# Ten dependent steps of a reciprocal root kept together on the vector engine by a list scheduler, and the load of the vector c moved ahead of that of x

## The chip, the core and the metric

The kernel runs on one core of one Trainium2 chip. TensorE (PE) multiplies, VectorE (DVE) and ScalarE (ACT) work on elements, GpSimd (POOL) takes some of the element work too, and SyncE (SP) issues every DMA. The metric is the device time of one execution in microseconds, the median of several runs.

## What is computed

Two transformer blocks of two layers each, one after the other, for 512 tokens of 1024 features in fp32. The first has two gated feed-forward parts around a mixer (sliding-window attention, a linear recurrence, a short convolution); the second has latent attention and then neighbourhood attention over tokens and a context, each with a convolutional feed-forward part. Every part is preceded by a norm over the features, and the shifts, scales and gates around it are products of the vector c with large matrices. Two of the norms, cut to what matters:

```python
def rmsnorm(x, g):
    xf = x.astype(jnp.float32)
    y = xf * lax.rsqrt(jnp.mean(xf * xf, axis=-1, keepdims=True) + EPS)
    return (y * g.astype(jnp.float32)).astype(x.dtype)

def first_block(x, c, w_mod, b_mod, g_norm, ...):
    c_act = jax.nn.silu(c)
    for l in range(DEPTH):
        mod = (c_act @ w_mod[l] + b_mod[l]).reshape(c.shape[0], N_MOD, D_MODEL)
        h = modulate(x, g_norm[l, 0], mod[:, 0], mod[:, 1])
        x = x + 0.5 * mod[:, 2][:, None, :] * swiglu(h, w_ffn1_gu[l], w_ffn1_down[l])
        ...

def layer_norm(x, g, b):
    mu = jnp.mean(xf, -1, keepdims=True)
    var = jnp.mean(jnp.square(xf - mu), -1, keepdims=True)
    return ((xf - mu) * lax.rsqrt(var + LN_EPS)).astype(x.dtype) * g + b
```

## The kernel before

Features lie along the 128 partitions and tokens along the free axis, so x is eight tiles of 128 by 512. Each fp32 matrix is split into a high and a low part (`wh` written by ACT, `wl` by DVE; in the same way `hh`, `hl` for activations), and each product is three matmuls. The weights come by DMA in blocks of 128 by 512 (`wr`), and the rows of the matrices that are multiplied by c come as `mr`.

The program isn't issued as it is written. `Recorder` takes it down op by op and `schedule` makes a list schedule from estimated costs: each engine takes the earliest op of the program whose operands are there and whose tiles have room. `emit` then issues all ops in that order (line 429 in the profile), and on the chip each engine runs its own list strictly in order. DVE and ACT are `PATIENT`: they leave a ready op alone for a moment if an op that stands earlier in the program becomes ready within `WAIT`, 70 ns of the schedule's clock. The schedule lets 135 ns pass between a DVE op and a DVE op that uses its result.

A norm is made for half of the tokens at a time (256; in a few places all 512). Sums over the features go through PE (`ps<-ones,acc`), then DVE has the variance `v` of each token as a column of 128 by 2 (or 4). `rsqrt` works on these columns in ten steps, each of which needs the one before: a first guess by integer arithmetic, and three Newton rounds of three ops. In the profile they are the DVE rows `c<-c` and `c<-c,c` (first the one with int32). PE then turns the column over and spreads it (`ps<-ident,c`, `bcast`), and DVE multiplies x by it. I call the ten steps a chain; the program has 27 of them, and they are numbered in order of time. In the second block's layer norms the mean is subtracted too: `x<-x,bm`, of eight tiles three on DVE and five on POOL. PE's list also holds other products, which lie before and behind the transposes of a norm as the schedule has them.

At the start, `setup` loads the eight tiles of x, then c in two halves spread over the partitions (`load_c`, tiles `b_c`, with a Silu on ACT), then the constants; `first_mods` multiplies the first rows of the matrices by c on DVE and POOL.

Of the kernel before, what the change touches and what calls it, by code (L numbers as in the profile page):

```python
# [69 lines left out]


def parts(T):
    """The tokens in halves: a norm over one runs beside the products of the other."""
    return [slice(i, i + C) for i in range(0, T, C)]


# [9 lines left out]


class View:
    """A part of a tile that gets its memory once the order of the program is known."""

    __slots__ = ("t", "box", "ops", "flat", "raw", "size")

# [37 lines left out]


class Op:
    __slots__ = ("eng", "calls", "acc", "cost", "func", "deps", "after", "succ", "begun", "need", "ready", "news", "frees", "prio", "start")


class Engine:
# [13 lines left out]


class Recorder:
    """Takes the program down op by op, then issues it in the order of a list schedule: each engine
    runs the earliest op of the program whose operands are there and whose tiles have room."""

    ENGINES = ("tensor", "vector", "scalar", "gpsimd", "sync")
    LAT = {"tensor": {"tensor": 0},
# [4 lines left out]
    FROM_PE, FROM_DMA, DMA_LAT, FREE, TO_DMA = 200, 130, 2000, 100, 300  # L162
    LOOK, LOOK_DMA = 1400, 600
    PATIENT, WAIT, SHORT = ('vector', 'scalar'), 70, 1000

    def __init__(self, nc, pools):
        self.nc, self.pools = nc, pools
        self.ops = []
        self.open = None
        self.pe = self.ve = 0.0  # L170
        self.later = 0
        for e in self.ENGINES:
            setattr(self, e, Engine(self, e))

# [32 lines left out]
    def call(self, eng, method, a, k):  # L207
        also = [(v, True) for v in k.pop("also", ())]
        outs = [a[0]] + [k[x] for x in ("accum_out",) if x in k]
        ins = [x for x in list(a[1:]) + [v for n, v in k.items() if n != "accum_out"] if isinstance(x, View)]  # L210
        acc = [(v, True) for v in outs if isinstance(v, View)] + [(v, False) for v in ins] + also
        func = a[2] if method == "activation" else None
        item = (method, a, k)
        cost = self.cost(eng, method, a, k)
        if eng == "tensor":
            self.pe += cost
        elif eng == "vector":
            self.ve += cost
        if self.open is not None:
            if self.open:  # L220
                o = self.open[0]
                o.calls.append(item)
                o.acc += acc
                o.cost += cost
                return
        o = Op()
        o.eng, o.calls, o.acc, o.cost, o.func = eng, [item], acc, cost, func
        o.prio = len(self.ops) + self.later
        if self.open is not None:
            self.open.append(o)  # L230
        self.ops.append(o)
# [53 lines left out]
    def schedule(self):  # L285
# [69 lines left out]
        while remaining:  # L355
            for e in self.ENGINES:
                if busy[e]:
                    continue
                f = future[e]
                while f and f[0][0] <= now:  # L360
                    offer(heapq.heappop(f)[2])
                best = None
                for h in avail[e].values():
                    if h and (best is None or h[0] < best[0]) and room(h[0][1], ops[h[0][1]]):
                        best = h
                if best is None or e in self.PATIENT and any(
                        r <= now + self.WAIT and p < best[0][0] and ops[i].cost < self.SHORT for r, p, i in f[:8]):
                    continue
                pick = heapq.heappop(best)[1]
                o = ops[pick]  # L370
                for g in [g for t in o.news for g in t.tags]:
                    live[g] += 1
                    if pick > cursor:
                        load[g][cursor:pick] += 1
                cost = o.cost
                if o.func is not None:
                    s = ACT_SETS.get(o.func)
                    if s is not None and s != table:
                        if not (s == "exp" and table == "sig" and o.func == AF.Tanh):
                            table = s  # L380
                            cost += 1300
                o.start = now
                order.append(pick)
                busy[e] = True
                for j in o.begun:
                    release(j, now)
                seq += 1
                heapq.heappush(events, (now + cost, seq, pick, 0))
# [41 lines left out]


class Lag:
    """Puts the parts of a chain that wait for other engines behind the start of the next ones."""

    def __init__(self, n):
        self.n, self.q = n, []
# [17 lines left out]
class Core:  # L454
# [45 lines left out]
    def setup(self):  # L500
# [7 lines left out]
        nc.vector.memset(mean, 1.0 / D)  # L508
        nc.scalar.copy(self.mean, mean)
        self.cb = {}  # L510
        self.x = []
        for m in range(KD):
            t = self.t(s="x")
            self.nc.sync.dma_start(t, self.io["xT"][m * P:(m + 1) * P, :])
            self.x.append(t)
        self.load_c(0, "c")
        self.gn = self.load_const("gnorm")
        self.bmod = self.load_const("bmod")
        self.mods = self.cst([P, 264], "mods")
# [104 lines left out]
                    self.mcol[(kind + sfx, l, ch)] = cols  # L624

    def first_mods(self):
        """The first shift and scale, finished block by block of features."""
        nc = self.nc
        Sh, G = self.mods[:, 0:8], self.mods[:, 8:16]
        for m in range(8):  # L630
# [86 lines left out]

    def rsqrt(self, v, n):
        nc = self.nc
        y, q = self.col(n), self.col(n)  # L720
        nc.vector.tensor_scalar(y.bitcast(I32), v.bitcast(I32), -0.5, float(0x5F3759DF), op0=ALU.mult, op1=ALU.add)
        for _ in range(3):
            nc.vector.tensor_tensor(q, y, y, op=ALU.mult)
            nc.vector.scalar_tensor_tensor(q, q, -0.5, v, op0=ALU.mult, op1=ALU.mult)
            nc.vector.scalar_tensor_tensor(y, q, 1.5, y, op0=ALU.add, op1=ALU.mult)
        return y

    def bcast(self, col, T, copy=None):
# [6 lines left out]
        return copy[:, :T]  # L735

    def times(self, p, c):
        """Weights of a softmax times their sum's reciprocal."""
        self.nc.gpsimd.tensor_scalar(p, p, c, 1.0, op0=ALU.mult, op1=ALU.mult)

    def rms(self, x, T, width, eps=1e-6):
# [65 lines left out]
        yield from self.ffn_end(x, dn, prev, hid, gate, T, after)  # L807

    def ffn_end(self, x, dn, prev, hid, gate, T, after):
        """The products with the last two groups of hidden features, for half the tokens and then the others."""  # L810
        gate = self.mod(*gate)
        last = len(FF_CHUNKS) - 1
        a, b = {}, {}
# [39 lines left out]
        return o  # L853

    def run(self, main, side):
        """Takes main down; between its steps, a step of the modulations for every `every` ns of tensor
        work and steps of side up to `share` of main's tensor work."""
        rec = self.nc
        mods, own = BEGIN, 0.0
        due = 0.0  # L860
# [15 lines left out]
            mark = rec.pe  # L876

    def rms_part(self, l, sub):
        """The modulated norm before a sublayer of the first block, for some of the tokens at a time."""
        out = [self.pair(S, "h") for _ in range(KD)]  # L880

        def part(sl):
# [7 lines left out]
        return out, part  # L890

    def final_part(self):
        """The first block's last norm, then the second block's first modulation."""
        nc = self.nc
        out = [self.pair(S, "a") for _ in range(KD)]
        g = self.gn[:, 48:56]
# [189 lines left out]
                yield from after(sl)  # L1086

    def stack(self, hi, lo):
        """For two heads' halves of 64 rows: each head's high and low parts over one another."""
        nc = self.nc  # L1090
        n = hi.width()
        other = self.t(F32R, s="st")[:, :n]
# [3 lines left out]
        return hi, other  # L1096

    def twice(self, hi):
        """For two heads' halves of 64 rows: each head's rows two times over."""
        nc = self.nc  # L1100
        n = hi.width()
        other = self.t(F32R, s="tw")[:, :n]
# [3 lines left out]
        return hi, other  # L1106

    def mm2x(self, outs, qs, ks, lows):
        """Products of two heads: q's both parts with k's high part in one pass, its high part with
        k's low part in the other."""  # L1110
        te = self.nc.tensor
        rows = (slice(0, 64), slice(64, 128))
        self.nc.group()
        for o, q, k in zip(outs, qs, ks):
            te.matmul(o, q, k, start=True, stop=False)
        for o, q, r in zip(outs, qs, rows):
            te.matmul(o, q[r], lows[r], start=False, stop=True)
        self.nc.group()
# [64 lines left out]
        return output  # L1183

    def centre(self, x, T):
        """Shifts each token by about the mean of its features: a layer norm, which follows, is the
        same for any shift, and its variance loses no digits to a large mean."""
        nc = self.nc
        acc = self.total(x, T, dt=F32R)
        bc = self.ps()[:, :T]  # L1190
# [2 lines left out]
            nc.vector.tensor_tensor(x[k], x[k], bc, op=ALU.subtract)  # L1193

    def ln_part(self, xs, T, l, which, kind, mod, perm=False):
        """A layer norm, and the modulation after it, for some of the tokens at a time."""
        nc = self.nc
        n = C // P
        c0 = (l * 2 + which) * 16
# [61 lines left out]
        return View(b[0][0].t, (0, P, 0, 512)), View(b[0][1].t, (0, P, 0, 512)), b[0][2]  # L1261

    def values(self, cn, wv, ts):
        """Values of 8 heads for 128 tokens: for each head its high and low parts side by side, the
        other way round for odd heads, so that the high parts' rows are the head's own."""
        nc = self.nc
        pv = self.ps()
        for k in range(2):
# [267 lines left out]
            nc.sync.dma_start(View(self.rpbt.t, (0, 16 * P, 24 * cq, 24 * cq + 24), raw=out), View(ed.t, ed.box, raw=inp))  # L1536

    def na_values(self, g, a, ac):
        """Values of two pairs of heads, tokens along the partitions: the four blocks of the latent
        tokens, the three that lie half a block further, and the context's two."""  # L1540
        nc = self.nc
        ws = [self.wblk("nqkv", 12 * g + i) for i in range(4)]
        wide = [tuple(View(w[j][part].t, (0, P, j * P, j * P + 256), (("__getitem__", ((slice(0, P), slice(j * P, j * P + 256)),), {}),))
# [282 lines left out]
```

## Time and profile before

| | |
|---|---|
| median of three runs | 3641.77 us (3635.7 to 3643.74) |
| span of the profiled execution, first to last instruction | 3637.0 us |
| PE busy | 3507.4 us, 96% of the span |
| DVE busy | 2715.5 us, 75% |
| ACT busy | 1822.0 us, 50% |
| POOL busy | 794.7 us, 22% |
| DMA | 469.86 MB, 129 GB/s on average |

For the profiled execution the page gives the span alone; it lies 4.8 us under the median of the runs and within their spread. PE's share is an average: in the slices of the page it lies at nine tenths nearly everywhere but at the start. DVE has stretches with no idle time beside long ones with a third of it. PE waits where another engine's result is late, and the rows name that engine.

### The profile page before, as it was taken

Reading aid. Unit: us, or ns where it says so; the run is one execution under the profiler, and the core shown is the slowest. Engines: PE = TensorE matmul, PEld = TensorE weight load, DVE = VectorE, ACT = ScalarE, POOL = GpSimd, SP = SyncE. Lnnn points to the kernel's source line nnn. Section 1 sums busy time; section 2 is a strip of 40 time slices with the busy share of each in tenths; the row PEclk is TensorE's granted clock in tenths of the full one; section 3 lists DMA queues with packets and bytes.
Section 4 is the critical chain, followed back from the end, with each engine's and each line's share of the span. In section 5 each row is a group of like instructions: output and inputs, shape, how many; then the busy total and the mean of one; then the engine's idle time right before and its main releaser. Section 6 shows DMA issues by size and latency. Waiting matters only on the chain.

```text
span 3637.0 us, 56958 instructions
## 1 busy us (share of the span) xinstructions
PE 3507.4 (96%) x19814; PEld 3057.1 (84%) x19814; DVE 2715.5 (75%) x5566; ACT 1822.0 (50%) x3939; POOL 794.7 (22%) x848
## 2 busy tenths in 40 slices
PE   6999999999999999999999999999999899989998
PEld 5888979878898879889888988888888888878887
DVE  8966799976597776986444589998667767786566
ACT  5434466455455644754333479785344444454332
POOL 3301142421022330230000034342000523240002
PEclk9999999999999999999999999999999999989999
DMA  9954254655356543553335322124333133233320
GB/s 316 312 157 148 82 184 148 218 182 162 103 191 197 187 132 119 193 160 116 105 108 143 107 59 58 48 68 133 110 96 105 53 100 85 76 94 103 98 87 24
DMA packets 272127, 469.86 MB, mean 129 GB/s; under 512 B 39136, under 2 KB 53472, under 8 KB 271840
## 3 DMA queue, kind: packets, MB, share of 16 engines
q1 hardware_dynamic: 271840, 466.23, 41.9%
q8 instruction: 156, 2.56, 0.3%
q14 instruction: 131, 1.07, 0.1%
HBM read 448.81 MB, written 5.50 MB: 125 GB/s over the span
## 4 chain that ended last, share of the span: by engine, by line
PE 79%; DVE 13%; issue 2%; ACT 2%; DMA 2%; POOL 1%; SPq 0%; POOLq 0%; DVEq 0%; ACTq 0%
PE ps L429 79%; DVE wl L429 2%; DVE c L429 2%; DVE mr L429 1%; DVE acc L429 1%; DVE x L429 1%; DVE mj L429 1%; DVE ptl L429 1%; DMA mr<-in_wmod 1%; POOL P L429 0%; DMA wr<-in_gu 0%; DVE pl L429 0%; DVE al L429 0%; POOL pc L429 0%; DVE yl L429 0%
## 5 line engine op out<-in xcount | busy, mean ns | idle before, releaser
L429 DVE TENSOR_TENSOR wl<-wr,wh 128x512 fp32r<-128x512 f32 (+1 forms) x1182 | 834.4, 729 | 163.0 <-ACT wh L429 134.1
L429 ACT CAST wh<-wr 128x512 fp32r<-128x512 f32 (+1 forms) x1182 | 676.6, 614 | 96.0 <-PE ps L429 61.2
L429 PE MATMUL ps<-hh,wh 128*128 128x512 f32 (+1 forms) x1864 | 692.9, 372 | 3.3 <-ACT wh L429 2.7
L429 PE MATMUL ps<-hl,wh 128*128 128x512 f32 (+1 forms) x1864 | 689.7, 370 | 6.3 <-DVE hl L429 6.2
L429 PE MATMUL ps<-hh,wl 128*128 128x512 f32 (+1 forms) x1864 | 688.0, 369 | 0.1
L429 PE MATMUL ps<-fh,wh 128*128 128x512 f32 (+1 forms) x1344 | 463.5, 345 | 0.0
L429 PE MATMUL ps<-fl,wh 128*128 128x512 f32 (+1 forms) x1344 | 462.0, 344 | 0.2 <-DVE fl L429 0.2
L429 PE MATMUL ps<-fh,wl 128*128 128x512 f32 (+1 forms) x1344 | 461.8, 344 | 0.0
L429 PEld LDWEIGHTS ps<-hl,wh 128*128 128x128 f32 x1864 | 355.4, 191 | 65.0 <-DVE hl L429 9.3
L429 PEld LDWEIGHTS ps<-hh,wh 128*128 128x128 f32 x1864 | 355.5, 191 | 60.8 <-ACT wh L429 3.1
L429 PEld LDWEIGHTS ps<-hh,wl 128*128 128x128 f32 x1864 | 355.1, 190 | 59.7 <-DVE wl L429 1.3
L429 DVE SCALAR_TENSOR_TENSOR x<-ps,mods,x 128x512 f32<-128x512 f32 (+1 forms) x400 | 254.9, 641 | 187.8 <-PE ps L429 186.1
L429 PE MATMUL ps<-ah,wh 128*128 128x512 f32 (+1 forms) x1000 | 366.9, 367 | 0.0
L429 PE MATMUL ps<-al,wh 128*128 128x512 f32 (+1 forms) x1000 | 365.3, 365 | 0.1
L429 PE MATMUL ps<-ah,wl 128*128 128x512 f32 (+1 forms) x1000 | 364.9, 365 | 0.0
L429 POOL TENSOR_TENSOR mr<-mr,b_c 128x512 f32<-128x512 f32 x123 | 179.0, 1457 | 515.1 <-DMA mr<-in_wmod 247.6
L429 DVE SCALAR_TENSOR_TENSOR cv<-ps,ffc,cv 128x511 f32<-128x511 f32 (+1 forms) x264 | 173.3, 659 | 143.7 <-ACT cv L429 140.1
L429 PEld LDWEIGHTS ps<-fl,wh 128*128 128x128 f32 x1344 | 254.7, 190 | 30.0 <-DVE fl L429 0.4
L429 PEld LDWEIGHTS ps<-fh,wl 128*128 128x128 f32 x1344 | 254.6, 189 | 30.1
L429 PEld LDWEIGHTS ps<-fh,wh 128*128 128x128 f32 x1344 | 254.7, 189 | 29.5
L429 ACT ACTIVATE cv<-ps,ffc 128x512 f32<-128x512 f32 (+1 forms) x132 | 93.4, 708 | 314.7 <-PE ps L429 314.0
L429 ACT CAST fh<-s 128x512 fp32r<-128x512 f32 x132 | 81.8, 621 | 299.1 <-DVE s L429 297.0
(332 smaller groups left out, 7115.6 us busy)
## 6 DMA issues: line engine op xcount, KB each, us to landing
wr<-in_gu SPq DMA_DIRECT2D x352, 256.0 KB, 2.9
mr<-in_wmod SPq DMA_DIRECT2D x288, 256.0 KB, 4.2
wr<-in_fin SPq DMA_DIRECT2D x264, 256.0 KB, 2.7
mr<-in_wada SPq DMA_DIRECT2D x192, 256.0 KB, 3.6
wr<-in_dn SPq DMA_DIRECT2D x176, 256.0 KB, 3.1
wr<-in_fout SPq DMA_DIRECT2D x132, 256.0 KB, 2.7
wr<-in_win SPq DMA_DIRECT2D x64, 256.0 KB, 3.3
wr<-in_nqkv SPq DMA_DIRECT2D x48, 256.0 KB, 2.9
```

The source lines that it names most:

```text
L429: getattr(eng, method)(*a, **k)
```

## The change

`rsqrt` marks its ops as urgent. Where an op of the engine's own list will be ready soon, the schedule waits for it up to 260 ns if it is urgent, and 70 ns otherwise. All urgent ops are DVE's, so ACT's own choices are made by the same rule as before. In `setup` the call of `load_c` stands ahead of the loads of x. Some comments are gone as well, by which line 429 becomes 433.

```diff
     PATIENT, WAIT, SHORT = ('vector', 'scalar'), 70, 1000
+    URGENT = 260
...
         o.prio = len(self.ops) + self.later
+        o.urgent = self.urgent
...
                 if best is None or e in self.PATIENT and any(
-                        r <= now + self.WAIT and p < best[0][0] and ops[i].cost < self.SHORT for r, p, i in f[:8]):
+                        r <= now + (self.URGENT if ops[i].urgent else self.WAIT) and p < best[0][0] and ops[i].cost < self.SHORT
+                        for r, p, i in f[:8]):
                     continue
...
         self.cb = {}
+        self.load_c(0, "c")
         self.x = []
         for m in range(KD):
             t = self.t(s="x")
             self.nc.sync.dma_start(t, self.io["xT"][m * P:(m + 1) * P, :])
             self.x.append(t)
-        self.load_c(0, "c")
...
     def rsqrt(self, v, n):
         nc = self.nc
+        nc.urgent = True
         y, q = self.col(n), self.col(n)
         nc.vector.tensor_scalar(y.bitcast(I32), v.bitcast(I32), -0.5, float(0x5F3759DF), op0=ALU.mult, op1=ALU.add)
         for _ in range(3):
             nc.vector.tensor_tensor(q, y, y, op=ALU.mult)
             nc.vector.scalar_tensor_tensor(q, q, -0.5, v, op0=ALU.mult, op1=ALU.mult)
             nc.vector.scalar_tensor_tensor(y, q, 1.5, y, op0=ALU.add, op1=ALU.mult)
+        nc.urgent = False
         return y
```

Over the whole program 144 other DVE instructions stood between the first and the last step of the 27 chains; now 19 do (4 in the first chain, 6 each in chains 7 and 18, 3 in two others). What this does to DVE's list is shown at chain 26, in the last layer norm, for the first half of the tokens. Here `c_39358` is the variance, `c_39367` the root as it comes, `c_39371` the helper; `x` are tiles of x, `bm` the mean, `ps_...` with `mods` a product that is added to x. Before:

```order
L429 TENSOR_TENSOR x_98<-x_98,bm_39369 128x256
L429 SCALAR_TENSOR_TENSOR c_39367<-c_39371,c_39367 128x2
L429 TENSOR_TENSOR x_107<-x_107,bm_39369 128x256
L429 TENSOR_TENSOR c_39371<-c_39367 128x2
L429 TENSOR_TENSOR x_119<-x_119,bm_39369 128x256
L429 SCALAR_TENSOR_TENSOR c_39371<-c_39371,c_39358 128x2
L429 SCALAR_TENSOR_TENSOR x_103<-ps_39338,mods,x_103 128x256
L429 SCALAR_TENSOR_TENSOR c_39367<-c_39371,c_39367 128x2
L429 TENSOR_TENSOR c_39371<-c_39367 128x2
L429 SCALAR_TENSOR_TENSOR c_39371<-c_39371,c_39358 128x2
L429 SCALAR_TENSOR_TENSOR c_39367<-c_39371,c_39367 128x2
L429 SCALAR_TENSOR_TENSOR x_105<-ps_39387,mods,x_105 128x256
```

And now (the x tiles have other numbers, since c is loaded first):

```order
L433 SCALAR_TENSOR_TENSOR c_39367<-c_39371,c_39367 128x2
L433 TENSOR_TENSOR c_39371<-c_39367 128x2
L433 SCALAR_TENSOR_TENSOR c_39371<-c_39371,c_39358 128x2
L433 SCALAR_TENSOR_TENSOR c_39367<-c_39371,c_39367 128x2
L433 TENSOR_TENSOR c_39371<-c_39367 128x2
L433 SCALAR_TENSOR_TENSOR c_39371<-c_39371,c_39358 128x2
L433 SCALAR_TENSOR_TENSOR c_39367<-c_39371,c_39367 128x2
L433 TENSOR_TENSOR x_105<-x_105,bm_39369 128x256
L433 TENSOR_TENSOR x_112<-x_112,bm_39369 128x256
L433 TENSOR_TENSOR x_123<-x_123,bm_39369 128x256
L433 TENSOR_TENSOR ln_39416<-x_105,ps_39405 128x256
```

The three subtractions `x<-x,bm` and one sum `x<-ps,mods,x` that stood inside the chain now stand behind it, the subtractions ahead of the products `ln<-x,ps`.

PE's list changes with it, since the schedule now counts on an earlier end of the chain. These are the rows around the transposes of chain 26, before:

```order
L429 MATMUL ps_39387<-fh_39003,wh_38794 128x256
L429 MATMUL ps_39387<-fl_39008,wh_38794 128x256
L429 MATMUL ps_39387<-fh_39003,wl_38818 128x256
L429 MATMUL ps_39387<-fh_39078,wh_38809 128x256
L429 MATMUL ps_39387<-fl_39087,wh_38809 128x256
L429 MATMUL ps_39387<-fh_39078,wl_38830 128x256
L429 MATMUL ps_39387<-fh_39160,wh_38809 128x256
L429 MATMUL ps_39387<-fl_39168,wh_38809 128x256
L429 MATMUL ps_39387<-fh_39160,wl_38830 128x256
L429 MATMUL ps_39419<-ident,c_39367 128x128 x2
L429 MATMUL ps_39424<-fh_38545,wh_38822 128x256
```

And now:

```order
L433 MATMUL ps_39388<-fh_38945,wh_38794 128x256
L433 MATMUL ps_39388<-fl_38952,wh_38794 128x256
L433 MATMUL ps_39388<-fh_38945,wl_38818 128x256
L433 MATMUL ps_39405<-ident,c_39367 128x128 x2
L433 MATMUL ps_39388<-fh_39003,wh_38794 128x256
L433 MATMUL ps_39388<-fl_39008,wh_38794 128x256
L433 MATMUL ps_39388<-fh_39003,wl_38818 128x256
L433 MATMUL ps_39388<-fh_39078,wh_38809 128x256
L433 MATMUL ps_39388<-fl_39087,wh_38809 128x256
L433 MATMUL ps_39388<-fh_39078,wl_38830 128x256
L433 MATMUL ps_39388<-fh_39160,wh_38809 128x256
```

The transposes, which wait for the chain's last step, stand nine matmuls earlier; the nine that stood ahead of them follow behind. The other transposes of a chain are moved forward in the same way, by 0 to 69 matmuls, but for one, which is moved back by 36. At the sums over the features that each half of a norm begins with, the lists of most norms agree again.

SP issues the DMAs in this order at the start, before (ahead of these rows six more tiles of x):

```order
L429 DMA x_119<-in_xT 128x512
L429 DMA x_125<-in_xT 128x512
L429 DMA b_c_131<-in_cvec 128x512
L429 DMA b_c_136<-in_cvec 128x512
L429 DMA gnorm<-in_gnorm 128x56
```

And now (five more tiles of x follow, then `gnorm`):

```order
L433 DMA b_c_98<-in_cvec 128x512
L433 DMA b_c_103<-in_cvec 128x512
L433 DMA x_105<-in_xT 128x512
L433 DMA x_107<-in_xT 128x512
L433 DMA x_110<-in_xT 128x512
```

The two halves of c are the first two transfers and not the ninth and tenth; from the eleventh on the list is as before, up to the 86th.

## Rows read from the trace of the kernel before

**Rows 1.** The page's first line.
```profile
span 3637.0 us, 56958 instructions
```

**Rows 2.** Whom PE waited for, whole span: us in total, times, longest us.
```profile
PE ps L429 <- DVE c L429: 35.8, 16, 9.9
PE ps L429 <- DVE mods L429: 10.5, 1, 10.5
```

**Rows 3.** Tile c: count, ns min/median/max, first and last start us, forms.
```profile
L429 DVE TENSOR_SCALAR c<-c x116: 137/163/1265, 14.0 to 3623.3; 128x2 f32<-128x2 f32 x80, 128x2 int32<-128x2 int32 x24, 128x4 f32<-128x4 f32 x9, 128x4 int32<-128x4 int32 x3
```

**Rows 4.** PE's same wait in 388:736, 736:2440, 2440:3615 and 3615:3637 us.
```profile
PE ps L429 <- DVE c L429: 15.5, 3, 9.9
...
PE ps L429 <- DVE c L429: 3.0, 3, 2.3
...
PE ps L429 <- DVE c L429: 12.1, 9, 2.4
...
PE ps L429 <- DVE c L429: 5.3, 1, 5.3
```

**Rows 5.** Windows: length, busy us of each engine, granted clock, DMA share, GB/s.
```profile
0.00:61.00 61.00, 30.15 (x100) 21.84 (x100) 51.60 (x93) 29.66 (x62) 27.32 (x25) 1.00 0.99 347
388.00:736.00 348.00, 322.47 (x1928) 284.57 (x1928) 335.18 (x786) 197.96 (x482) 125.33 (x99) 0.97 0.52 165
```

**Rows 6.** DVE in order of time, 2077 to 2080 us: start us, us, instruction.
```profile
2077.85 0.17 DVE L429 TENSOR_SCALAR c<-c 128x2 int32<-128x2 int32 x1
...
2079.42 0.36 DVE L429 SCALAR_TENSOR_TENSOR c<-c,c 128x2 f32<-128x2 f32 x2
```

**Rows 7.** DVE in order of time, 3602 to 3608 us.
```profile
3602.38 0.17 DVE L429 TENSOR_SCALAR c<-c 128x2 int32<-128x2 int32 x1
...
3604.02 0.69 DVE L429 SCALAR_TENSOR_TENSOR c<-c,c 128x2 f32<-128x2 f32 x1
...
3606.52 0.47 DVE L429 SCALAR_TENSOR_TENSOR x<-ps,mods,x 128x256 f32<-128x256 f32 x1
...
3607.51 0.36 DVE L429 SCALAR_TENSOR_TENSOR c<-c,c 128x2 f32<-128x2 f32 x2
```

**Rows 8.** POOL in order of time, 3603 us.
```profile
3603.08 4.19 POOL L429 TENSOR_TENSOR x<-x,bm 128x256 f32<-128x256 f32 x5 [2.56 <-ACT bm L429]
```

**Rows 9.** PE in order of time, 3605 to 3608 us; in brackets the wait.
```profile
3605.78 0.28 PE L429 MATMUL ps<-fl,wh 128*128 128x256 f32 x1
3605.90 0.28 PE L429 MATMUL ps<-fh,wl 128*128 128x256 f32 x1
3607.92 0.43 PE L429 MATMUL ps<-ident,c 128*128 128x128 f32 x2 [1.74 <-DVE c L429]
```

**Rows 10.** DVE in order of time at the end, 3626 to 3630 us.
```profile
3626.79 1.36 DVE L429 SCALAR_TENSOR_TENSOR c<-c,c 128x2 f32<-128x2 f32 x2
...
3629.51 2.74 DVE L429 TENSOR_TENSOR ln<-x,ps 128x256 f32<-128x256 f32 x8 [0.78 <-PE ps L429]
```

**Rows 11.** DVE in order of time near the start.
```profile
13.19 0.69 DVE L429 SCALAR_TENSOR_TENSOR mr<-mr,b_c 128x512 f32<-128x512 f32 x1 [2.16 <-DMA mr<-in_wmod]
...
14.00 1.18 DVE L429 TENSOR_SCALAR c<-c 128x4 int32<-128x4 int32 x1
```

**Rows 12.** ACT in order of time near the start.
```profile
8.96 0.63 ACT L429 ACTIVATE sq<-x 128x512 f32<-128x512 f32 x1 [0.35 <-DMA x<-in_xT]
...
11.22 1.38 ACT L429 ACTIVATE b_c<-b_c 128x512 f32<-128x512 f32 x2 [0.34 <-DMA b_c<-in_cvec]
```

**Rows 13.** PE in order of time: the first transposes, and those at 735 us.
```profile
23.51 1.09 PE L429 MATMUL ps<-ident,c 128*128 128x128 f32 x4 [10.55 <-DVE mods L429]
...
735.20 0.69 PE L429 MATMUL ps<-ident,c 128*128 128x128 f32 x2 [9.92 <-DVE c L429]
```

**Rows 14.** The chain that ended last, first 63 us: start us, us, what.
```profile
59.79 1.53 DVE hl L429
```

**Rows 15.** DVE in order of time, 413 us: two steps of chain 3.
```profile
413.18 2.42 DVE L429 SCALAR_TENSOR_TENSOR c<-c,c 128x2 f32<-128x2 f32 x2
```

More of the change, by code (lines that the diff above doesn't have):

```diff
@@ L132 @@
 class Op:
-    __slots__ = ("eng", "calls", "acc", "cost", "func", "deps", "after", "succ", "begun", "need", "ready", "news", "frees", "prio", "start")
+    __slots__ = ("eng", "calls", "acc", "cost", "func", "deps", "after", "succ", "begun", "need", "ready", "news", "frees", "prio", "start", "urgent")
 class Engine:
@@ L171, in __init__ @@
         self.later = 0
+        self.urgent = False
         for e in self.ENGINES:
```

## The prediction

> **What bounds the kernel now.** I begin with the span [rows 1] and then ask whom PE waits for, since it is busy for nearly all of it. Over the whole span PE waits 35.8 us for DVE's small columns `c`, in 16 waits, and once 10.5 us for `mods` [rows 2]. Nearly all of the first sum is one thing: transposes that wait for the last step of a chain. There are 27 chains (24 on columns of 128x2, 3 on 128x4) [rows 3]. At most 35.8 us, 1.0% of the span, can come from the waits that carry the chain's name, and 10.5 more if the first transposes, whose releaser is named `mods`, count too.
>
> By stretches the same wait is 15.5 us from 388 to 736 us (three waits), 3.0 from 736 to 2440, 12.1 from 2440 to 3615 (nine waits), and 5.3 in the last 22 us [rows 4]. Between 61 and 388 us there is none. The reader should then look at what DVE does meanwhile: from 388 to 736 us it is busy for 335.2 of 348 us, more than PE's 322.5 [rows 5]. There the limit is DVE itself: the longest wait, 9.92 us at 735 us [rows 13], ends when DVE has worked off its list. In the first 61 us DMA engines are busy for 0.99 of the time and DVE for 51.6 us [rows 5], and what PE waits for at the end of it, at 61 us, is DVE's last `hl` [rows 14].
>
> **What one chain costs.** Where nothing else stands in it and POOL is idle, it takes 1.93 us, from 2077.85 to 2079.42 + 0.36 [rows 6]; so a step is 0.16 or 0.17 us long and follows the one before after 0.195. Chain 26, with four other ops in it, runs from 3602.38 to 3607.51 + 0.36, which is 5.49 us [rows 7]. If the other ops were all, it would come down by 3.56. But not all of the time is theirs: some steps take 0.69 us in place of 0.17 [rows 7], just while POOL's five subtractions run from 3603.08 for 4.19 us [rows 8]. Are these long steps a matter of what is put between? In chain 27, the next one, two steps that follow each other directly take 1.36 us together [rows 10], and near the start single steps on their own take 1.18 us beside larger POOL ops [rows 11]. So I take it that a chain kept together still meets each of POOL's five ops once: five steps of 0.68, five of 0.17 and nine pauses of 0.03 make 4.5 us, a gain of about 1.0 and not of 3.56. From here I use 1.1, since the steps before POOL begins are the same.
>
> The Trainium skill says the same in general (SBUF — State Buffer, "Who interferes with whom"): a Vector op with two SBUF inputs and a GpSimd op that reads SBUF exclude each other for the whole instruction, and which was issued first decides who waits. The trace agrees with its 0.69 against 0.17 us. By that rule each chain that waits between its steps opens the port to POOL ten times; without it the gain per chain would be 3.56 us.
>
> **Part 1: what PE's order takes back.** The schedule thinks the chain ends earlier and puts the transposes earlier too. For chain 26 they stand nine matmuls forward, at 0.12 us each [rows 9] 1.08 us. PE waits 1.74 us there [rows 9]. After the change it comes to the transposes 1.08 us sooner and the chain ends 1.1 us sooner, so it waits 1.7 us again and nothing is won; if the chain ended 3.56 us sooner, the whole wait would be gone. This is the sum for each chain: the earlier end of the chain less the matmuls moved behind, and never more than the old wait.
>
> From 2440 to 3615 us seven chains are waited for (20 to 26). Their transposes move by 51 matmuls together, nine of them (chain 21's) twice as wide: 42 x 0.12 + 9 x 0.24 = 7.2 us. The chains end 7 x 1.1 = 7.7 us earlier, and a little more where a chain held more than chain 26 did (chain 20 held nine ops, but now has six sums of another norm ahead of it). I take a gain of 1.0, between 0 and the whole 12.1.
>
> From 736 to 2440 us three chains are waited for. One loses ten ops ahead of its end and 39 matmuls ahead of its transposes, the others four ops and three matmuls, or four and nine. I take 1.0 of the 3.0.
>
> At the end, chain 27 has no matmul to fill with: PE's transposes keep their place, so the 1.1 us count. The three subtractions that stood inside come behind; two lie in DVE's wait of 0.78 us for the transposes [rows 10], the third costs about 0.33. Gain 0.8, with bounds of 0 and 3.56.
>
> The chains that nobody waits for (2, 4, 8, 11, 13 to 19) I cost at nothing: PE has other products there. Were that cover gone, each would pay or gain about what chain 26 does.
>
> **Part 2: from 388 to 736 us.** DVE's work is the same, only in another order, and DVE sets the end. Five chains (3 to 7) lie there. Each may add some 0.3 us of pauses where it had none: 5 x 0.3 = 1.5 us more. Against this stand DVE's 12.8 us of idle time [rows 5], which the ops put off by chains 3 and 4 can fill in part; two or three microseconds. I take 0, from -4 to +4. A shorter wait at an earlier transposes is worth nothing here, since it comes back at 735 us.
>
> **Part 3: c ahead of x.** The last square of x begins at 8.96 us, when its x has come, and the Silu of c at 11.22 us, when c has [rows 12]. The first half of c thus takes the queue 2.3 us behind x; with the second half I allow 3 us, by which x comes later when c is first. No op on c gains by it: DVE's first product with c, at 13.19 us, waits for the matrix's rows `mr` and not for c [rows 11], and these rows keep their place behind both. The chain begins later by up to 3 us, loses 3 other ops from inside and gets 4, and its steps still meet POOL (1.18 us, [rows 11]). But PE starts in earnest only at 61 us, behind DVE's list of the same work, so a delay of the chain is only felt as far as DVE idles more than the 2.16 us that it waits at 13.19 already [rows 11]. I take 0, from -1 to +3.
>
> **The sum.** 1.0 + 1.0 + 0.8 + 0 + 0 = 2.8 us less. The span of 3637.0 lies 4.8 under the median of the runs; the change of 2.8 is taken off the median, 3641.8 - 2.8 = 3639.0, no change that can be measured: 0.2%, 7.3 us, is about what a measurement of this kernel can tell.
>
> **Rivals.**
> - *POOL does not get in.* The steps stay at 0.17 us, and chains take 1.93. Then every wait after 736 us goes, since 3.56 us is more than any moved matmuls (of chain 26: 1.08) and waits but the last: 3.0 + 12.1 + 3.5 = 18.6, or 3623 us. For it: chains at 2077 us show it possible. Against it: where PE waits, POOL's subtractions start from the same mean. Half of it, with some steps met, gives about 3632.
> - *POOL takes the time from DVE where DVE has none.* From 388 to 736 us a step met by POOL costs 1.18 - 0.17 = 1.0 us, as near the start. POOL is busy 125.3 of 348 us there [rows 5], 36%; of the five chains' 50 steps that would be 18. Two of chain 3's are met already (2.42 us for the two) [rows 15]; 16 more make 3639 + 16 = 3655. It decides from eleven more on. The rule above speaks for it: a DVE that waits leaves the port free. Against it: a POOL op that does not meet a step meets another op of DVE instead.
> - *The start costs what the rest brings.* c holds up x by 3 us and with it the first `hl` and the long stretch of PE; 3639 + 3 = 3642, no change either.
> - *Nothing but order moves*, so that PE's waits only shift to the next sums: 3641.8, part of the same case.
>
> **Chances.** My forecast 0.46, the start and mere shifts 0.10, POOL kept out, wholly or in half, 0.30, POOL in DVE's stretch 0.14. So faster by over 0.2% 0.30, within 0.2% 0.56, slower 0.14. The forecast's own range is 3633 to 3645 (Part 1 between 0 and 6, Part 2 by 4 each way). To leave out no more than 2 in 10 I go to 3625, nearly to the first rival, and to 3648, short of the second.
>
> **What would show it.** Right: chain 26 at some 4.5 us, steps of 0.68 while POOL subtracts, PE's waits for `c` from 2440 to 3615 us still some 11 us in sum, and a wait of about 10 at the transposes that now stands at 735 us. Wrong on the fast side: chains near 2 us in the layer norms, and that sum under 4. Wrong on the slow side: more steps over 1 us between 388 and 736 us, or PE's long stretch beginning after 64 us. What I can't read from the rows is how often POOL and DVE meet once their timing shifts.

## The result, and the profile after

The changed kernel takes 3655.58 us (median of four runs, 3652.61 to 3660.68) against 3640.47 us of four runs of the kernel before beside it. The ratio on record is 1.0051, 95% interval 1.0039 to 1.0063; the two medians alone divide to 1.0042. It is slower by about half a per cent, outside the range of 3625 to 3648 us.

The page's first lines; in brackets each engine's share of the span [rows 1]:

```profile
span 3658.5 us, 56899 instructions
...
PE 3519.8 (96%) x19814; PEld 3064.8 (84%) x19814; DVE 2722.1 (74%) x5566; ACT 1820.0 (50%) x3937; POOL 797.0 (22%) x848
```

The span is 21.5 us longer. PE does the same number of matmuls, and 12.4 of the 21.5 us are PE's busy time: the same work took longer. The other 9.1 us are idle time of PE. Whom PE waits for in the changed kernel, over the whole span (us in total, times, longest):

```profile
PE ps L433 <- DVE c L433: 35.3, 13, 9.1
...
PE ps L433 <- DVE wl L433: 6.8, 5, 2.8
...
PE ps L433 <- DVE pl L433: 5.6, 6, 2.4
...
PE ps L433 <- DVE al L433: 2.9, 7, 1.0
PE ps L433 <- POOL pl L433: 2.7, 2, 2.4
...
PE ps L433 <- DMA qh<-ql: 2.5, 3, 1.7
PE ps L433 <- ACT fh L433: 2.2, 1, 2.2
...
PE ps L433 <- DVE fl L433: 1.9, 1, 1.9
...
PE ps L433 <- ACT ah L433: 1.4, 2, 1.3
PE ps L433 <- DVE V L433: 1.4, 1, 1.4
```

The wait for `c` now includes the first transposes (8.0 us), whose wait stood under `mods` before, so 35.3 us answer to 35.8 + 10.5 = 46.3 [rows 2]: the chains brought 11.0 us. The reader should see what follows below: `wl` was 2.2 us before, `pl` 2.4, `al` 0.5, `fl` 0.2; the others had no row. (`acc`, the second row of the whole list, is 31.6 us and was 28.5.) The list gave back more than it won, at operations that have nothing to do with a reciprocal root.

The chains themselves are as short as they were made to be. Chain 26 on DVE (start us, us, instruction) [rows 7]:

```profile
3625.13 0.17 DVE L433 TENSOR_SCALAR c<-c 128x2 int32<-128x2 int32 x1
...
3625.92 0.66 DVE L433 TENSOR_TENSOR c<-c 128x2 f32<-128x2 f32 x1
3626.61 1.35 DVE L433 SCALAR_TENSOR_TENSOR c<-c,c 128x2 f32<-128x2 f32 x2
3628.00 0.65 DVE L433 TENSOR_TENSOR c<-c 128x2 f32<-128x2 f32 x1
3628.68 0.84 DVE L433 SCALAR_TENSOR_TENSOR c<-c,c 128x2 f32<-128x2 f32 x2
```

and POOL beside it [rows 8]:

```profile
3625.82 3.49 POOL L433 TENSOR_TENSOR x<-x,bm 128x256 f32<-128x256 f32 x5 [2.56 <-ACT bm L433]
```

It takes 4.40 us in place of 5.49, with five steps of about 0.67 us while POOL subtracts. Now PE in order of time, first the transposes that wait for chains 3, 6 and 26, then the places of the new waits (in brackets the wait and what ended it) [rows 9, 13]:

```profile
412.13 0.43 PE L433 MATMUL ps<-ident,c 128*128 128x128 f32 x2 [2.52 <-DVE c L433]
...
741.95 0.69 PE L433 MATMUL ps<-ident,c 128*128 128x128 f32 x2 [9.14 <-DVE c L433]
...
3629.58 0.43 PE L433 MATMUL ps<-ident,c 128*128 128x128 f32 x2 [1.74 <-DVE c L433]
...
592.40 0.39 PE L433 MATMUL ps<-a,wl 128*128 128x256 f32 x1 [2.82 <-DVE wl L433]
...
669.45 0.79 PE L433 MATMUL ps<-fh,wh 128*128 128x512 f32 x1 [2.22 <-ACT fh L433]
672.10 0.79 PE L433 MATMUL ps<-fl,wh 128*128 128x512 f32 x1 [1.85 <-DVE fl L433]
...
1520.66 0.30 PE L433 MATMUL ps<-kh,qh 128*128 128x128 f32 x1 [1.79 <-issue]
...
2144.71 0.50 PE L433 MATMUL ps<-wh,cnh 128*128 128x512 f32 x1 [1.37 <-DVE V L433]
...
2168.39 1.54 PE L433 MATMUL ps<-ident,pl 128*128 128x128 f32 x6 [2.41 <-POOL pl L433]
...
2471.13 0.38 PE L433 MATMUL ps<-ah,wh 128*128 128x256 f32 x1 [1.27 <-ACT ah L433]
```

PE waits 1.74 us for chain 26 as before: PE comes sooner by as much as the chain ends sooner. And the wait for chain 6 is 9.14 us, not 9.92, but it ends 6.75 us later.

To see where the time went, the two traces are laid beside each other: at points where both PE lists have issued the same matmuls, the start of the same matmul after, less that before. Its change over a stretch is what the stretch lost (+) or won (-). The first column is the changed kernel; the others are experiments that follow below.

| stretch of the kernel before, us | changed kernel | six chains urgent | the other 21 urgent | all 27 moved | six moved | nine moved |
|---|---|---|---|---|---|---|
| 0 to 387 | -0.7 | +1.3 | -0.8 | -0.2 | 0.0 | -0.7 |
| 387 to 742 | +8.6 | +4.9 | +3.4 | +3.8 | +6.2 | +1.0 |
| 742 to 1310 | -3.9 | -0.4 | -4.4 | -4.5 | -0.5 | -4.1 |
| 1310 to 1638 | +6.2 | +6.5 | +3.0 | +1.2 | +2.9 | 0.0 |
| 1638 to 2118 | 0.0 | 0.0 | 0.0 | 0.0 | 0.0 | 0.0 |
| 2118 to 2290 | +7.8 | +9.5 | 0.0 | +1.9 | +1.7 | +0.1 |
| 2290 to 2440 | +0.2 | -2.1 | -1.8 | -1.9 | -1.9 | -1.8 |
| 2440 to 2500 | +5.7 | +7.4 | +0.3 | +4.9 | +3.1 | +0.1 |
| 2500 to the end | -2.1 | -2.8 | -8.9 | -13.1 | -5.5 | -11.4 |

In the changed kernel four stretches lose 28.3 us, which lie behind chains 3 to 6, 12, 17 and 18, and 19; the others win 6.5. Each trace is a single execution: that of before spans 3637.0 us, where the spans of its 58 runs beside the experiments have medians of 3633.3 to 3633.9. Its half-speed stretches at 2295, 2919, 3189 and 3220 us are partly missing from the others, which is most of what the rows from 2290 to 2440 and from 2500 on show alike in columns with and without the chain's change. So a column's total is good to some 6 us, and verdicts go by the timed ratios.

### The profile page after: what moved, and what is told of

Read it like the earlier page. It is cut to its first block, busy times and chain, and to the rows that moved or that the text cites. A ratio compares the mean times of both kernels' runs of the same rounds, so it can differ in the third digit from the quotient of the medians.

```text
span 3658.5 us, 56899 instructions
## 1 busy us (share of the span) xinstructions
PE 3519.8 (96%) x19814; PEld 3064.8 (84%) x19814; DVE 2722.1 (74%) x5566; ACT 1820.0 (50%) x3937; POOL 797.0 (22%) x848
## 4 chain that ended last, share of the span: by engine, by line
PE 67%; DVE 9%; ACT 2%; issue 1%; DMA 1%; POOL 1%; SPq 0%; DVEq 0%; POOLq 0%; ACTq 0%
PE ps L433 67%; DVE c L433 1%; DVE wl L433 1%; DVE acc L433 1%; DVE mr L433 1%; DVE x L433 1%; DVE ptl L433 1%; DVE pl L433 0%; DMA mr<-in_wada 0%; DVE mj L433 0%; DVE al L433 0%; POOL pc L433 0%; ACT tm L433 0%; DVE os L433 0%; POOL pl L433 0%
```

## The experiments

Three theories stood at the start. A: the urgent steps are harmless where they stand, and the loss comes from the rest of the list, which is laid anew and laid worse. B: DVE's time is the price; what is pushed behind a chain comes late for PE right there. C: the load of c. Each kernel was timed beside the kernel before on the same chip, and each ratio is against that; what such a ratio is worth in us is reckoned from 3635 us.

**The two halves of the change.** The run `e1_urgent_only` takes the load back:

```diff
-        self.load_c(0, "c")
         self.x = []
...
             self.x.append(t)
+        self.load_c(0, "c")
```

> The change without its second part: c is loaded behind x again, the ten steps stay urgent. Theory A (the urgent steps are harmless or a small gain where they stand; the loss comes from the rest of the list, which the schedule lays anew, and from where other operations then come late for PE): as slow as the whole change, about 3654 us. Theory B (DVE's time is the price: work that is pushed behind the kept-together steps comes late for PE right there): the same, about 3654 us. Theory C (the loss comes from c ahead of x, which moves the start): 3640 us or less.

Measured: 3655.09 us, ratio 1.0049 (1.0036 to 1.0062). The run `e2_c_first` makes only this edit the other way round in the kernel before:

> The kernel before with c loaded ahead of x and nothing else; PE's and POOL's lists are those of before. Theories A and B: within 3 us of before, 3638 to 3643 us, and PE's long stretch begins within 2 us of 61 us. Theory C: 3650 us or more.

Measured: 3635.31 us, ratio 0.9995 (0.9986 to 1.0004). The whole loss is that of the urgent steps, and C falls.

**The chain kept together, and nothing else moved.** `e3_gather` leaves the schedule of before, and moves the chain's steps only in the finished list:

```diff
-        for i in self.schedule():
+        for i in self.gather(self.schedule()):
...
+    def gather(self, order):
+        steps = {}
+        for i in order:
+            steps.setdefault(self.ops[i].chain, []).append(i)
...
+            elif steps[c][0] == i:
+                out += steps[c]
```

> The kernel before with its schedule made as before; only then the steps of each of the 27 chains are moved up to stand directly behind the chain's first step. No other operation changes its place in any list but that DVE's 144 foreign operations come behind the chain. Theory A: PE's waits for c fall from 35.8 us to about 22, the new waits for wl, fl, al, pl and the like of the changed kernel are not there, and the time is 3624 to 3634 us. Theory B: those waits are there as in the changed kernel (wl 6.8, pl 5.6, al 2.9 us), and the time is 3648 us or more. From 388 to 736 us, where DVE is the bound, A expects no change beyond 3 us.

Measured: 3635.29 us, ratio 0.9996 (0.9987 to 1.0005). Neither theory has its number. PE's waits, whole span:

```profile
PE ps L446 <- DVE c L446: 24.9, 8, 9.5
...
PE ps L446 <- ACT yh L446: 5.3, 2, 3.2
...
PE ps L446 <- ACT hh L446: 4.1, 5, 1.4
PE ps L446 <- DVE pl L446: 2.2, 4, 0.8
PE ps L446 <- DVE wl L446: 2.2, 1, 2.2
```

The wait for `c` falls to 24.9 from 46.3 us, the first transposes included, twice what the changed kernel won, since here PE's transposes keep their place. The new waits for `wl` and `pl` aren't there, as A expected. But `hh` and `yh` are waited for instead (0.6 and 2.1 us before), as B expected. DVE behind chain 19:

```profile
2450.78 0.36 DVE L446 SCALAR_TENSOR_TENSOR c<-c,c 128x2 f32<-128x2 f32 x2
2451.05 1.10 DVE L446 TENSOR_TENSOR x<-x,bm 128x256 f32<-128x256 f32 x3
2452.18 0.42 DVE L446 TENSOR_TENSOR os<-os,ps 64x256 f32<-64x256 f32 x1
...
2453.08 0.43 DVE L446 TENSOR_TENSOR yl<-os,yh 128x256 fp32r<-128x256 f32 x1
```

and PE at the same place:

```profile
2453.10 0.58 PE L446 MATMUL ps<-yh,wh 128*128 128x256 f32 x1 [3.20 <-ACT yh L446]
```

`os` and `yl`, which stood in chain 19 before (at 2448.29 and 2450.27 us), come behind it; `yh` needs `os`, and PE, which came to `yh,wh` without a wait at 2449.40 us before, waits 3.20 us. In the timed runs the gain at the other chains and such prices cancel; that they do so place by place is not shown, since the trace is of an execution of 3631.11 us.

**Is it the chain at all?** `e4_wait68` and `e6_wait72` change a number of the schedule that means nothing on the chip, in the kernel before (the second has 72):

```diff
-    PATIENT, WAIT, SHORT = ('vector', 'scalar'), 70, 1000
+    PATIENT, WAIT, SHORT = ('vector', 'scalar'), 68, 1000
```

> The kernel before with the schedule's patience set from 70 to 68 ns, a change that means nothing on the chip: the chains keep as many foreign operations as before (140 for 144), but about as many rows of PE's list change their place as in the changed kernel (509 against 587). Theory A: the time is another draw, some 4 to 15 us away from before in either direction, with PE waiting at other places. Theory B: nothing that delays DVE's other work has changed, so within 5 us of before.

Measured: 3655.47 us, ratio 1.0049 (1.0036 to 1.0062), as slow as the change.

> The kernel before with the patience at 72 in place of 70 ns; the chains hold as many foreign operations as before (143 for 144), 240 rows of PE's list change their place. If each laying of the list is a draw and that of before a lucky one: slower, by 5 to 20 us. If 68 ns was slow for a reason of its own: within 5 us of before.

Measured: 3644.33 us, ratio 1.0026 (1.0015 to 1.0037). Two nanoseconds of patience either way cost 18 and 9 us with the chains all but untouched (140 and 143 other operations in them for 144): the list of before is the best of three draws. By the same comparison of traces, at 68 ns the losses lie elsewhere than in the changed kernel: +5.5 us from 440 to 578, +1.6 at 1300 where the change gained 3.0, and nothing from 2118 to 2290.

So the changed kernel could be just one bad draw. `e7_after72` and `e8_after68` set the same numbers in the changed kernel:

> The changed kernel (urgent steps, c first) with the patience at 72 ns: the chains stay together (19 foreign operations), 152 rows of PE's list change place against the changed kernel's. If the changed kernel's loss is that of one laying of the list, another laying gives another time, 5 us or more away from 3655 in either direction. If the loss belongs to the urgent steps: 3655 us again, within 3 us, with PE's waits for wl, fh, fl and pl.

> The changed kernel with the patience at 68 ns; 311 rows of PE's list change place against the changed kernel's, the chains stay together. Expected as with 72 ns: another time, 5 us or more away from 3655, if it is the laying of the list; 3655 within 3 us if it is the urgent steps. Against the kernel before at 68 ns (3655 us) it shows what the urgent steps are worth in another pair.

Measured: 3656.77 us, 1.0059 (1.0047 to 1.0071), and 3658.53 us, 1.0070 (1.0057 to 1.0083). With urgent steps all three lists are slow, within 0.2% of each other, and the urgent list is the slower one in each pair: at 70 ns by 0.5%, at 72 by 0.33%, and at 68 by 0.21%, where the two intervals still touch. Three pairs are few, so the times alone don't rule out a draw. The places speak more clearly. In all three traces the same stretches lose (665 to 700 us by 6.8, 6.9 and 7.3 us, 1480 to 1638 by 6.0, 5.5 and 8.6), and from 665 to 700 us neither list of 68 or 72 ns without urgent steps loses anything. Something in the urgent lists is laid late each time, and A as a mere draw falls there.

**Which chains.** Behind six chains the changed kernel lost. `e9_urgent_not6` makes the other 21 urgent, `e10_urgent_6` these alone, and `e11_gather_6` moves only these in the finished list of before. The edit of the first; the second has `in` for `not in`:

```diff
-        nc.urgent = True
+        nc.chains += 1
+        nc.urgent = nc.chains not in (4, 5, 12, 17, 18, 19)
```

> The changed kernel, but chains 4, 5, 12, 17, 18 and 19 are not urgent, those behind which the changed kernel's trace loses time on the one before (578 to 700, 1480 to 1638, 2118 to 2290, 2440 to 2500 us). The other 21 are urgent. If the loss belongs to how the schedule lays the list behind those six chains: the losses are gone and only the gains at chains 3, 9, 10, 11 and 27 are left, 3626 to 3634 us, or 0.9975 to 0.9995 of before. If any new laying of the list costs something wherever it is: slower than before by 3 to 10 us.

Measured: 3639.50 us, ratio 1.0009 (1.0001 to 1.0018). The loss is nearly gone, but the gain that was expected isn't there. (Its column in the table shows more than that, but is of an execution of 3629.44 us.)

> The changed kernel with only chains 4, 5, 12, 17, 18 and 19 urgent. If the loss belongs to these: 18 to 27 us slower than before, 1.005 to 1.0075, at the same places as in the changed kernel. If not: within 5 us of before.

Measured: 3660.66 us, ratio 1.0067 (1.0053 to 1.0081), as expected. The table has the loss from 1310 to 1638, 2118 to 2290 and 2440 to 2500 us at the size of the changed kernel's or larger. From 388 to 742 us it comes in another form (PE's waits in this stretch):

```profile
PE ps L434 <- DVE c L434: 21.1, 3, 16.3
PE ps L434 <- POOL P L434: 5.3, 6, 2.5
PE ps L434 <- ACT vf L434: 1.4, 1, 1.4
PE ps L434 <- DVE acc L434: 1.2, 2, 1.0
```

There is no wait for `wl`, `fh` or `fl`, but 16.3 us for chain 6: DVE is later by the end of the stretch, and PE pays there what it didn't pay on the way.

> The kernel before with its schedule as it was, and only then the steps of chains 4, 5, 12, 17, 18 and 19 moved together; PE's, ACT's and POOL's lists are those of before. It shares with the run that makes these six urgent that DVE's other operations come behind the chain, and not that the rest of the list is laid anew. If the loss is the laying of the rest: within 3 us of before. If it is the displaced operations: 15 us or more slower. From the traces of the kernel with all 27 moved and of the changed kernel I expect both, 8 to 12 us for the displaced operations (behind chains 4, 5, 17 and 19) and the other half for the laying, so 1.002 to 1.0035.

Measured: 3645.21 us, ratio 1.0030 (1.0020 to 1.0039). The same six chains kept together cost 0.30% where nothing else moves, and 0.67% where the list is laid anew around them: 10.9 us for displaced work, which is theory B, and 13.4 us more for the laying, which is theory A. The second figure and that of `e9_urgent_not6` come from one list each, and one list can be 18 us from another by a number that means nothing (`e4_wait68`), so their size is not firm. Their place is firmer: from 2118 to 2290 us the five lists with these six chains urgent (the changed kernel, `e1_urgent_only`, `e7_after72`, `e8_after68`, `e10_urgent_6`) lose 4.7 to 9.5 us, and the other lists between nothing and 3.5.

**The part that pays.** `e5_gather_sel` moves only chains 9, 10 and 21 to 27 in the finished list, where PE waits for the chain and nobody for what it displaces:

```diff
+        moved = {self.ops[i].chain for n, i in enumerate(first, 1) if n in (9, 10) or n > 20}
```

> As with all 27 chains moved together behind a finished schedule, but only chains 9, 10 and 21 to 27, the nine places where PE's list gained with all 27 moved (together some 11 us by the two traces). PE's list is that of before. Theory A (a chain that is kept together helps where PE waits for it, if nothing else in the list moves): PE's wait for c falls by about 10 us, and the time by 8 to 13 us, to 0.9965 to 0.998 of before. Theory B (DVE's displaced operations make PE wait as long elsewhere): no change, within 0.1%.

Measured: 3628.69 us, ratio 0.9984 (0.9976 to 0.9993): faster than the kernel before, by 5.8 us and not by 8 to 13. PE's wait at chains 22 and 26, each 1.74 us before:

```profile
2847.96 0.43 PE L446 MATMUL ps<-ident,c 128*128 128x128 f32 x2 [0.69 <-DVE c L446]
...
3592.22 0.43 PE L446 MATMUL ps<-ident,c 128*128 128x128 f32 x2 [0.69 <-DVE c L446]
```

The wait falls by 1.05 us, the chain's whole gain, since PE's order is left as it was. Part of what the chains win is waited for again one step later: for the sums that chain 23 starts from PE now waits 7.4 us, and 6.29 before.

## Why the prediction was wrong, step by step

- **One chain kept together: right.** 1.0 to 1.1 us was forecast for chain 26, and 5.49 - 4.40 = 1.09 came. Where POOL subtracts from the same mean, chains take 4.33 to 4.46 us; fourteen others take 1.93 to 2.01. The Trainium skill's rule (SBUF — State Buffer, "Who interferes with whom"), an exclusive lock between a two-input Vector op and a GpSimd op that reads SBUF, agrees with the 0.66 against 0.16 us of the steps. Rival 1, POOL kept out, fell where PE waits.
- **Part 1, what PE's order takes back: right for the chains' own waits, wrong as a sum of stretches.** From 2500 to 3615 us a gain of 1.1 us came (the sum had 1.0 from 2440 on), and at the end 1.1 for 0.8. But from 2440 to 2500 us 5.7 were lost, so over the stretch that this term covers, 2440 to 3615 us, 4.6 were lost. The moved transposes eat the gain: moved alone with PE's list left as it was, the same chains bring the difference (`e5_gather_sel`). PE's waits for `c` from 2458 to 3637 us are 10.2 us, as the 11 forecast.
- **"The chains that nobody waits for ... I cost at nothing: PE has other products there": this step failed.** Chains 17 and 18 are in that list, and the stretch behind them cost 7.8 us; chains 12 and 19 (12 costed as a small gain, 19 at nothing) have 6.2 and 5.7 behind them. Nobody waited for the chain, but PE's other products wait for DVE's other work, which the schedule set at other times around it: `V`, `pl`, `ah`, `al`, `qh`. The sentence on the cover priced its loss at about one chain's, 1 us; it was 6 to 8, and 19.7 in the three stretches together. Moved alone (`e11_gather_6`) these chains cost 2.9, 1.7 and 3.1 us there, so the larger part came with the new laying of the list, which the prediction did not price at all.
- **Part 2, 388 to 736 us: mis-sized, 0 (-4 to +4) for +8.6 us.** The last of DVE's list sets the end, as forecast, and it came later. The stretch up to the transposes of chain 6, after (length, then busy us of PE, PEld, DVE, ACT, POOL) [rows 5]:

```profile
388.00:741.95 353.95, 325.43 (x1921) 285.85 (x1919) 338.49 (x772) 196.60 (x481) 127.72 (x99) 0.96 0.51 161
```

Up to the same transposes DVE was busy for 334.48 of 347.20 us before. So it has 4.0 us more work time and 2.7 us more idle time; the prediction had DVE's work the same and counted on the idle time being filled. With `e11_gather_6`, where chains 4 and 5 are the only ones of this stretch that move, these transposes come 6.3 us later as well, so the displaced work alone can do it.
- **Part 3, the load of c: right.** Nothing (0.9995 measured).
- **Rival 2 has the time, but not by the steps that it named.** It gave 3655 us, from sixteen more steps met by POOL between 388 and 736 us. The steps of the chains there, after (count; ns min, median, max):

```profile
L433 DVE SCALAR_TENSOR_TENSOR c<-c,c x32: 154/161/164, 388.3 to 742.6; 128x2 f32<-128x2 f32 x32
...
L433 DVE TENSOR_TENSOR c<-c x17: 154/161/1183, 388.1 to 744.9; 128x2 f32<-128x2 f32 x17
L433 DVE TENSOR_SCALAR c<-c x6: 169/169/1156, 387.8 to 742.0; 128x2 int32<-128x2 int32 x6
```

No step of the commonest form is longer than 164 ns. Of the others two in chain 3 were met, at 1.16 and 1.18 us, and before it was five in this stretch. What did come is the rival's own objection, that POOL then meets another operation of DVE. DVE's large operations from 388 us up to the transposes of chain 6, before and after (count, busy us, mean ns, idle time before):

```profile
L429 DVE TENSOR_TENSOR wl<-wr,wh 128x512 fp32r<-128x512 f32 x99 | 77.4, 804 | 0.1
L429 DVE SCALAR_TENSOR_TENSOR mj<-mr,b_c 128x512 f32<-128x512 f32 x56 | 43.9, 796 | 0.1
L429 DVE SCALAR_TENSOR_TENSOR mr<-mr,b_c 128x512 f32<-128x512 f32 x13 | 9.7, 766 | 0.0
```

```profile
L433 DVE TENSOR_TENSOR wl<-wr,wh 128x512 fp32r<-128x512 f32 x98 | 83.2, 876 | 0.1
L433 DVE SCALAR_TENSOR_TENSOR mj<-mr,b_c 128x512 f32<-128x512 f32 x56 | 46.5, 846 | 0.1
L433 DVE SCALAR_TENSOR_TENSOR mr<-mr,b_c 128x512 f32<-128x512 f32 x12 | 12.3, 1039 | 0.0
```

They take 11.0 us more for two operations fewer. Of these three groups and `mr<-mr,b_cc` together, 46 of 222 operations ran over 0.9 us and 33 of 224 before, every one of them while a POOL instruction ran. In the three other traces with all chains urgent it is 45, 46 and 48, in two more with the list of before (`e2_c_first`, and `e5_gather_sel` in this stretch) 32 and 34. Smaller operations ran shorter (`c<-c,c` has a mean of 161 ns for 252), so that 4.0 us of it are left in DVE's busy time. POOL thus takes time from DVE where DVE has none, as the rival said, by its large operations and not by the chains' steps. It is not the only way to the loss: `e11_gather_6` is as late at these transposes with 34 such operations.
- **The signs all said that the prediction was right.** Chain 26 takes 4.40 us, its steps 0.66, PE's later waits for `c` are 10.2 us, the wait for chain 6 is 9.14; no more long steps came, and PE's long stretch began no later (-0.7 us up to 387). They watched the chains and the start, and the loss lay where no sign was set.
- **Rival 4, "Nothing but order moves", was priced at zero.** That was the error behind the failed step. An order that merely moves is not free here: 2 ns of patience cost 0.26 and 0.49%.

What stays open: why the schedule lays the list late at each of these places (one is followed below), and why with `e11_gather_6` DVE is 3.8 us longer busy up to chain 6 though POOL meets no more of its large operations. The parts also don't add up simply: the six chains cost 0.67% and the other 21 0.09%, together more than the 0.51% of the change. Between 388 and 742 us this is plain, because there only the end of DVE's list counts.

## What to carry to other kernels

When a scheduler's rule is changed, its effect on the operations that it names and its effect on all the others have to be tried apart: move the operations in the finished list for the first, and change a number that means nothing for the second. Here that number alone was worth up to half a per cent, as much as the change, so a single run of a changed rule says little of the rule. Keep a chain together only where someone waits for its end and no one for what it displaces.

## What the runs showed of the hardware that was not expected

A wait of PE can cost more than its length, when the granted clock falls behind it. At 1520 us PE waits 1.79 us for a row of `kh,qh`. The profile names no releaser; the transfer of `qh` from `ql` lands just then, at 1515.02 + 5.6 = 1520.6 us. Here it is in the windows from 1508 to 1522 us before and after (KB, us from issue to landing):

```profile
qh<-ql SPq DMA_DIRECT2D x1, 128.0 KB, 3.8
```

```profile
qh<-ql SPq DMA_DIRECT2D x1, 128.0 KB, 5.6
```

It is issued at 1511.42 us before and 1515.02 after, and takes 1.8 us longer to land. Then the clock, in a window of the changed kernel right behind the wait (the last three columns: granted clock, DMA share, GB/s):

```profile
1522.60:1529.40 6.80, 6.80 (x19) 4.99 (x20) 6.77 (x22) 3.70 (x16) 1.28 (x1) 0.50 0.92 327
```

At 0.50, which is 1.2 of 2.4 GHz, PE gets through 19 matmuls in 6.80 us; the kernel before, at full clock in its window from 1518.6 to 1525.4 us, through 32, nearly all of them of 128x512, where six of the 19 are narrower. A wait of 1.8 us lost some 5 us in all, as the comparison of the traces has it (+4.8 us from 1514 to 1520, as before's times go). It recurs: in the four other lists where chain 12 is urgent PE waits 1.0 to 1.8 us at the same matmul, and the clock is at 0.50 behind it for 3.4 us (`e1_urgent_only`) or 6.8; in the traces where chain 12 isn't urgent it stays at 1.00 from 1505 to 1535 us. But not every wait does this. Behind the 2.82 us for `wl` at 592 us the clock of the changed kernel stays at 1.00 up to 602 us, and behind the 1.74 us for chain 26 up to 3640 us.

Over the whole program the mean granted clock is 0.985 and was 0.988, so 2 x 0.015 x 3658.5 = 110 us at half clock for 2 x 0.012 x 3637 = 87. Half of these 23 us is about 11, nearly all of PE's 12.4 us more busy time: by this estimate about half of the 21.5 us between the two traces is clock. The Trainium skill (TensorE: Matmul & The Clock Gate, "Terms") reckons the penalty in this way, the time at the lower rate times the share of pulses that are held back, and the trace agrees, with its 12.4 us beside 11.
